# Decoder layer on Trainium2: sample activations of the down stage loaded in three pieces and kept, a fourth sum of w_down made one stage earlier, w_out in another order

## The chip, the cores and the metric

The kernel runs on one core of a Trainium2 chip. TensorE (PE) multiplies matrices, VectorE (DVE), ScalarE (ACT) and GpSimd (POOL) do elementwise work, and SyncE (SP) issues the DMA transfers. Each engine works through its own queue in order, and an instruction starts when those of other engines or DMAs that it needs have signalled. The metric is the device time of one launch in microseconds; lower is better.

## The reference

One layer of a decoder for 1024 prompt tokens and 64 sample tokens, D_MODEL 1024, D_FF 2816. Only the end of the layer matters here:

```
mix = (g_conv * u_out + g_nsa * nsa) @ w_out           # 1024 x 1024
x   = x + g1 * mix
h   = rms_norm(x, ffn_norm_g) * (1 + sc2) + sh2
ffn = (silu(h @ w_gate) * (h @ w_up)) @ w_down         # 1024 x 2816, twice, and 2816 x 1024
y   = x + g2 * ffn
```

All data are fp32.

## The kernel before

Each fp32 operand of a matrix product is split in two parts: `hi`, a rounded copy made by ACT (L152), and `lo = src - hi`, made by DVE or POOL. A product `mm3` is three matmuls (L338, L339, L340: hi·hi, lo·hi, hi·lo). For the 64 sample tokens `mm2` (L343, L344) packs hi and lo of the activations side by side in one left operand of 128 columns.

The three stages at the end:

- **w_out.** `out_half(i, j)` makes 128 tokens (i = 0 to 7; i = 8 is the samples) of one half of 512 columns: 24 matmuls into a `pf` bank, DVE's L1599 (times g1) and L1600 (plus x), a store (L1606), ACT's square with a row sum. When j is 1 the row's norm follows (L1610, L252, POOL's L253) and x is scaled, half by ACT (L152) and half by DVE (L1616). `norm2(sg)` transposes 256 tokens on PE (L1644), applies scale and shift (ACT L1647, DVE L1649) and splits the result (DVE or POOL L158). `norm2s` does the samples.
- **Gate and up.** 22 blocks `t` of 128 columns; blocks kk and kk + 11 form a pair. The product of a 2 by 2 block matrix is made with 7 products instead of 8, so sums of operands are needed on both sides. `build(u)` makes those of the activations, u = 0 for the tokens of groups 0 and 1, u = 1 for groups 2 and 3: 8 subtractions in place (L1675 to L1678) and 4 splits in two views (L1681), for u = 1 a third view for the samples. The splits go to `tq` tiles that take the place of the weights of w_out: `quarter(u)` hands out those of column half u. `load_up(t)` loads four tiles of weights and makes their sums and splits (L1715 on DVE or POOL, L1722, L1723, L1725, L1733). Raw tiles go round a ring `w` of six buffers. Each pair also runs two generators in spare places between the products: `second(kk)` loads three tiles of w_down, makes their sum `t2` (two L1792) and stores it, and `sums(kk)` makes the sums of the activations for the down stage (L1779).
- **Down.** The same scheme with phases p = 1, 2, 6, 7, 5, 4, 3 of 11 steps kk, 12 matmuls each into four banks `p`. `raw_` loads one operand of 256 KB; `parts` splits it, hi on ACT (L152), lo on DVE or POOL (L1891). p = 7 and p = 5 load two tiles of w_down and subtract them (L1958, L1961); p = 4 loads one and `t2` and subtracts (L1964). In p = 1, 2, 7, 3 each kk has two more matmuls (L343, L344) for the samples, whose activations `sample(t)` loads (L1896), copies (ACT L152, `sa`) and splits (L1899): 44 times, each t twice. At the end of a phase its four banks are added to accumulators (ACT's copy after p = 1; DVE's L1998 after p = 6, L2000 after p = 7) and come free for the phase after next but one.

The order of the instructions on each engine is fixed when the program is built: a scheduler simulates the program as written and lists it by its own clock. Tiles with a tag share a ring of `bufs` buffers, and a tile's first write waits for the last use of the tile before it in that buffer.

The lines of the order of w_out, of `place` and of the phases stand below.

Of the kernel before, what the change touches and what calls it, by code (L numbers as in the profile page):

```python
# [123 lines left out]
def emit(tc, I, O):  # L124
    nc = tc.nc
# [1417 lines left out]

    NH = FF // 256
    act_d = {p: T(dp, [NH, 128, 512], f"act_d{p}") for p in range(1, 8)}
    acts_d = T(dp, [2 * NH, 128, 2, 32], "acts_d")
    t2_d = T(dp, [NH, 128, 512], "t2_d")

    def gate_rows(i, pool, tag, bufs):
        out = []  # L1550
# [74 lines left out]
    def place(sg):  # L1625

        u, r = sg // 2, sg % 2
        if r == 0:
            tb[u] = [[quarter(u) for _ in range(2)] for _ in range(4)]
        for a in range(2):  # L1630
            if sg == 0:
                full[u][a] = [T(ap_[0], [128, 2, 256], "aw", bufs=6) for _ in range(2)]
            else:
                x = T(mp, [128, 4, SEG[1 + r * u * 2]], ("qh0", "ql0")[a] + str(1 + r * u * 2))
                full[u][2 * r + a] = [x[:, 2 * b:2 * b + 2, :256] for b in range(2)]
# [30 lines left out]

    def build(u):

        views = [([t[a] for t in full[u]],
                  [[t[:, 2 * a:2 * a + 2, :256] for t in x] for x in tb[u]]) for a in range(2)]  # L1670
        if u:
            views.append(([xs[:, 4 * a:4 * a + 4, 32 * b:32 * b + 32] for a, b in ((0, 0), (1, 0), (0, 1), (1, 1))],
                          [[t[:, :, 256:] for t in x] for x in tb[u]]))
        for (b11, b21, b12, b22), dst in views:
            V.tensor_tensor(b11, b12, b11, op=ALU.subtract)  # L1675
            V.tensor_tensor(b12, b22, b12, op=ALU.subtract)
            V.tensor_tensor(b22, b22, b11, op=ALU.subtract)
            V.tensor_tensor(b21, b21, b22, op=ALU.subtract)  # L1678
            for src, j in ((b22, 1), (b12, 2), (b11, 0), (b21, 3)):
                acopy(dst[j][0], src)  # L1680
                V.tensor_tensor(dst[j][1], src, f(dst[j][0]), op=ALU.subtract)  # L1681

    for i in range(9):
        out_half(i, 0)
    for sg in (0, 1):
        for i in (2 * sg, 2 * sg + 1):
            out_half(i, 1)
        norm2(sg)
    build(0)
    out_half(8, 1)  # L1690

# [95 lines left out]
    def second(kk):  # L1787

        t2 = wd(kk + NH, 1, T(stg[0], [128, 512], "t2", bufs=2))
        for j, op_ in ((1, ALU.subtract), (0, ALU.add)):  # L1790
            b = wd(kk, j, T(fr, [128, 512], "w", bufs=6))
            V.tensor_tensor(t2, t2, b, op=op_)  # L1792
            yield
        nc.sync.dma_start(t2_d[kk], t2)

    todo = []

# [7 lines left out]
    for n_, t in enumerate([a + b for a in range(NH) for b in (0, NH)]):  # L1805
# [8 lines left out]
        for u in range(2):  # L1814
# [32 lines left out]
            if (u, t // NH) != (1, 0):  # L1847
                store({(0, 0): 1, (0, 1): 2, (1, 1): 4}[u, t // NH], kk, h)
            if u:
                nc.sync.dma_start(acts_d[t], h[:, :, 256:])  # L1850
        if t >= NH:
            todo.append(sums(kk))
    while todo:
# [18 lines left out]
    with ExitStack() as es:  # L1872
# [14 lines left out]
        def parts(src, e):  # L1887
# [3 lines left out]
            e.tensor_tensor(lo, src, f(hi), op=ALU.subtract)  # L1891
            return hi, lo

        def sample(t):
            sr = T(dn, [128, 64], "sr", bufs=8)
            nc.sync.dma_start(sr.rearrange("p (a c) -> p a c", a=2), acts_d[t])  # L1896
            sa_ = T(dn, [128, 128], "sa", F32R, bufs=8)
            acopy(sa_[:, :64], sr)
            V.tensor_tensor(sa_[:, 64:], sr, f(sa_[:, :64]), op=ALU.subtract)  # L1899
            return sa_  # L1900

        def load_x2(i, j):
            n = 128 if i < 8 else 64
# [29 lines left out]
        for p in (1, 2, 6, 7, 5, 4, 3):  # L1933
            pd_ = [T(psd, [128, 512], "p", bufs=7) for _ in range(4)]
            if p in (1, 7):
                ps_ = T(psd, [128, 512], "s", bufs=1)
            j, e = (0 if p < 3 else 1), (G if p in (4, 5, 7) else V)

            def step(n, kk, a, b, c):
                if n == 4:  # L1940
                    mm2(ps_, c[0], *c[1], p in (1, 7) and kk == 0, p in (2, 3) and kk == NH - 1)
                else:
                    mm3(pd_[n], a[0][:, n * 128:n * 128 + 128], a[1][:, n * 128:n * 128 + 128], *b,
                        kk == 0, kk == NH - 1)

            late = []
            order = ([4] if p in (1, 2, 7, 3) else []) + list(range(4))
            for kk in range(NH):
                l = raw_(act_d[p][kk])
                c = None  # L1950
                if p in (1, 2, 3):
# [8 lines left out]
                    o_, r = wraw_(kk, 1), wraw_(kk, 0)  # L1960
                    V.tensor_tensor(r, o_, r, op=ALU.subtract)  # L1961
                else:
                    o_, r = wraw_(kk + NH, 0), raw_(t2_d[kk])
                    V.tensor_tensor(r, o_, r, op=ALU.subtract)  # L1964
                a, b = parts(l, e), parts(r, V)
                if p in (1, 2, 3):
                    c = sample(kk + (NH if p > 1 else 0)), b
# [93 lines left out]
```

## Time and profile before

| | us |
|---|---|
| three runs | 1936.15, 1926.62, 1930.79 |
| median | 1930.79 |
| profiled execution | 1924.53 |
| its span | 1922.7 |

| engine | busy us | share |
|---|---|---|
| PE (matmul) | 1822.3 | 95% |
| PEld (weight load) | 1633.5 | 85% |
| DVE | 1479.6 | 77% |
| ACT | 858.5 | 45% |
| POOL | 713.4 | 37% |

The page divides the span into 40 slices. w_out ends and gate/up begins near 1177 us, the down stage runs from about 1645 us to the end. In the rows below a time is in microseconds from the start of the span, and L numbers are lines of the kernel before. `A<-B` is out<-in; a wait in brackets is the engine's idle time just before the row and what ended it.

### The profile page before, as it was taken

How to read it: one execution, taken by the hardware profiler on the slowest of the kernel's cores; microseconds unless marked ns; L12 is line 12 of the kernel's file. 1: busy time of each engine (PE TensorE's matmuls, PEld its weight loads, DVE VectorE, ACT ScalarE, POOL GpSimd, SP SyncE). 2: the span in 40 equal slices, each digit the busy share in tenths (PEclk: the TensorE clock that was granted, in tenths of full speed). 3: DMA queues.
4: the chain of work that ended last, by engine and by line, in shares of the span. 5: the costliest groups of instructions: out<-in, count | busy, mean ns of one | idle time of the engine just before them, and what ended most of it. 6: DMA issues, size and time to landing. Idle time of an engine off the chain costs nothing.

```text
span 1922.7 us, 32565 instructions
## 1 busy us (share of the span) xinstructions
PE 1822.3 (95%) x11432; PEld 1633.5 (85%) x11432; DVE 1479.6 (77%) x2698; ACT 858.5 (45%) x2086; POOL 713.4 (37%) x689
## 2 busy tenths in 40 slices
PE   8999899999999789999998997999999999999899
PEld 3889888888898589788888886999999999877687
DVE  4877799987958875898886538988777888767873
ACT  5434642344444342777784325433323323464440
POOL 3789421144544666555555403211111111002420
PEclk9989999999999889999999998999999999999999
DMA  9576534443454425110006712344433344596862
GB/s 314 181 228 214 164 113 144 140 149 115 150 171 138 155 85 176 55 47 6 1 7 196 225 47 71 106 140 122 123 113 112 111 130 129 181 303 217 277 225 77
DMA packets 228050, 271.86 MB, mean 141 GB/s; under 512 B 32297, under 2 KB 151609, under 8 KB 227814
## 3 DMA queue, kind: packets, MB, share of 16 engines
q1 hardware_dynamic: 218670, 236.22, 38.9%
q0 software_dynamic: 9216, 33.56, 5.2%
q8 instruction: 90, 1.47, 0.3%
q14 instruction: 74, 0.61, 0.1%
HBM read 215.68 MB, written 58.52 MB: 143 GB/s over the span
## 4 chain that ended last, share of the span: by engine, by line
PE 47%; DMA 4%; DVE 4%; issue 1%; POOL 1%; ACT 1%; SPq 0%; DVEq 0%; ACTq 0%; POOLq 0%
PE pf L338 6%; PE pf L340 6%; PE pf L339 6%; PE pt L340 3%; PE pt L339 3%; PE pt L338 3%; PE pT L1400 3%; PE p L338 3%; PE p L340 3%; PE p L339 3%; PE po L1407 2%; PE po L1408 2%; DMA raw<-in_w_down 2%; PE pS L1359 1%; PE pS L1361 1%
## 5 line engine op out<-in xcount | busy, mean ns | idle before, releaser
L338 PE MATMUL pd<-hh,whi 128*128 128x384 f32 (+1 forms) x576 | 192.4, 334 | 1.0 <-ACT stg L152 0.9
L340 PE MATMUL pd<-hh,wlo 128*128 128x384 f32 (+1 forms) x576 | 190.7, 332 | 0.8 <-DVE wlo L270 0.8
L339 PE MATMUL pd<-hl,whi 128*128 128x384 f32 (+1 forms) x576 | 190.5, 331 | 0.0
L1096 DVE SCALAR_TENSOR_TENSOR y<-U,wdT,y 128x1024 f32<-128x1024 f32 x120 | 163.2, 1360 | 0.6
L1715 POOL TENSOR_TENSOR aw<-s,aw 128x512 fp32r<-128x512 f32 x21 | 28.9, 1376 | 305.7 <-ACT aw L152 291.4
L152 ACT ACTIVATE whi<-wraw 128x512 fp32r<-128x512 f32 (+1 forms) x133 | 81.7, 626 | 92.5 <-PE pd L339 40.9
L152 ACT ACTIVATE aw<-w 128x512 fp32r<-128x512 f32 x133 | 83.0, 628 | 88.4 <-PE pf L339 55.5
L958 POOL TENSOR_TENSOR vv<-kraw,vv 128x256 fp32r<-128x256 f32 x80 | 92.3, 1178 | 67.7 <-ACT vv L152 67.6
L338 PEld LDWEIGHTS pd<-hh,whi 128*128 128x128 f32 x576 | 108.7, 189 | 7.6 <-ACT stg L152 1.2
L1388 POOL TENSOR_SCALAR P<-P,ast 128x640 f32<-128x640 f32 (+7 forms) x128 | 88.9, 715 | 70.5 <-DVE ast L1384 66.6
L1404 DVE TENSOR_TENSOR pl<-pT,ph 128x512 fp32r<-128x512 f32 (+1 forms) x148 | 99.2, 681 | 18.0 <-ACT ph L152 16.7
L340 PEld LDWEIGHTS pd<-hh,wlo 128*128 128x128 f32 x576 | 108.5, 188 | 3.9 <-DVE wlo L270 2.2
L339 PEld LDWEIGHTS pd<-hl,whi 128*128 128x128 f32 x576 | 108.6, 189 | 3.0 <-issue 0.5
L338 PE MATMUL pz<-whi,hh 128*128 128x256 f32 (+1 forms) x320 | 96.0, 301 | 14.9 <-ACT zt L152 13.2
L338 PE MATMUL pf<-tq,aw 128*128 128x256 f32 (+1 forms) x352 | 101.8, 289 | 3.5 <-ACT s L152 1.8
L338 PE MATMUL pt<-tq,aw 128*128 128x256 f32 (+1 forms) x352 | 101.9, 290 | 2.1 <-ACT aw L152 2.1
L340 PE MATMUL pt<-tq,aw 128*128 128x256 f32 (+1 forms) x352 | 101.7, 289 | 1.0 <-POOL aw L1715 1.0
L339 PE MATMUL pt<-tq,aw 128*128 128x256 f32 (+1 forms) x352 | 101.9, 290 | 0.0
L340 PE MATMUL pf<-tq,aw 128*128 128x256 f32 (+1 forms) x352 | 101.8, 289 | 0.0
L339 PE MATMUL pf<-tq,aw 128*128 128x256 f32 (+1 forms) x352 | 101.7, 289 | 0.0
L340 PE MATMUL pf<-qh,aw 128*128 128x256 f32 (+1 forms) x352 | 101.5, 288 | 0.0
L339 PE MATMUL pf<-ql,aw 128*128 128x256 f32 (+1 forms) x352 | 101.4, 288 | 0.0
(653 smaller groups left out, 6368.7 us busy)
## 6 DMA issues: line engine op xcount, KB each, us to landing
wraw<-in_w_in SPq DMA_DIRECT2D x68, 256.0 KB
wraw<-in_w_ada SPq DMA_DIRECT2D x64, 256.0 KB
w<-in_w_down SPq DMA_DIRECT2D x62, 256.0 KB
raw<-in_w_down SPq DMA_DIRECT2D x48, 256.0 KB
w<-in_w_gate SPq DMA_DIRECT2D x44, 256.0 KB
w<-in_w_up SPq DMA_DIRECT2D x44, 256.0 KB
raw<-act_d SPq DMA_DIRECT2D x42, 256.0 KB
w<-act_d SPq DMA_DIRECT2D x35, 256.0 KB
```

Of the source, the lines that this page charges most:

```text
L152: S.activation(out, in_, AF.Copy, scale=scale)
L338: PE.matmul(out, ah, bh, start=first, stop=False)
L339: PE.matmul(out, ah, bl, start=False, stop=False)
L340: PE.matmul(out, al, bh, start=False, stop=last)
L958: G.tensor_tensor(vv[:, :, 1], r, f(vv[:, :, 0]), op=ALU.subtract)
L1096: V.scalar_tensor_tensor(op, U[:, k:k + TP], wk, op, op0=ALU.mult, op1=ALU.add)
L1388: G.tensor_scalar(P_[br][g][:, :w], P_[br][g][:, :w], st[:, 2, br, g:g + 1], 1.0, op0=ALU.mult, op1=ALU.mult)
L1400: PE.transpose(pT[:nk, g * 128:(g + 1) * 128], a, ident)
L1404: V.tensor_tensor(pl_[:nk], pT[:nk], f(ph[:nk]), op=ALU.subtract)
L1407: PE.matmul(po, va, ph[:nk], start=(bi == 0), stop=False)
L1408: PE.matmul(po, va, pl_[:nk], start=False, stop=(bi == len(blocks) - 1))
L1715: e.tensor_tensor(lo, src, f(hi), op=ALU.subtract)
```

## The change

1. `acts_d`, the samples' activations in HBM, are laid out as [22, 128, 64]. `load_sample(t, n)` loads n blocks with one DMA, copies them with one ACT instruction and subtracts with one of DVE, into `sal`, which is kept for the whole stage. Three calls in p = 1, before kk = 0, 4 and 7, load 8, 8 and 6 blocks, and `sample(t)` is a view of `sal`.
2. `second(kk)` loads one more tile of w_down into the ring `w`, subtracts `t2` (new line L1800) and stores the result in `t4_d` (L1801). p = 4 loads it from there: its load of w_down and its L1964 are gone. The lo parts of its activations go from POOL to DVE (`e` is POOL for p = 5 and 7 alone).
3. w_out: the halves (0,1), (1,1), norm2(0), (2,1), (3,1), norm2(1) stand between the halves j = 0, and (7,0) and (8,0) stand just ahead of build(0). `tb[u]` is taken in `build` instead of `place`.

Instructions: DVE 2580 rows to 2549, ACT 1715 to 1673, POOL 666 to 656, SP 1089 to 1059, PE 10863 in both. Lines after 1546 move by one to 16: L1599, L1600, L1616, L1649 are L1600, L1601, L1617, L1648; L1681 stays; L1715, L1722, L1733, L1792, L1825 are L1719, L1726, L1737, L1796, L1832; L1891, L1961, L2000 are L1898, L1976, L2014.

```diff
@@ -1543,8 +1543,9 @@
 
     NH = FF // 256
     act_d = {p: T(dp, [NH, 128, 512], f"act_d{p}") for p in range(1, 8)}
-    acts_d = T(dp, [2 * NH, 128, 2, 32], "acts_d")
+    acts_d = T(dp, [2 * NH, 128, 64], "acts_d")
     t2_d = T(dp, [NH, 128, 512], "t2_d")
+    t4_d = T(dp, [NH, 128, 512], "t4_d")
 
     def gate_rows(i, pool, tag, bufs):
         out = []
@@ -1625,8 +1626,6 @@
     def place(sg):
 
         u, r = sg // 2, sg % 2
-        if r == 0:
-            tb[u] = [[quarter(u) for _ in range(2)] for _ in range(4)]
         for a in range(2):
             if sg == 0:
                 full[u][a] = [T(ap_[0], [128, 2, 256], "aw", bufs=6) for _ in range(2)]
@@ -1666,6 +1665,7 @@
 
     def build(u):
 
+        tb[u] = [[quarter(u) for _ in range(2)] for _ in range(4)]
         views = [([t[a] for t in full[u]],
                   [[t[:, 2 * a:2 * a + 2, :256] for t in x] for x in tb[u]]) for a in range(2)]
         if u:
@@ -1680,12 +1680,16 @@
                 acopy(dst[j][0], src)
                 V.tensor_tensor(dst[j][1], src, f(dst[j][0]), op=ALU.subtract)
 
-    for i in range(9):
+    for i in range(4):
         out_half(i, 0)
-    for sg in (0, 1):
-        for i in (2 * sg, 2 * sg + 1):
-            out_half(i, 1)
-        norm2(sg)
+    for i, j in ((0, 1), (1, 1), (4, 0)):
+        out_half(i, j)
+    norm2(0)
+    for i, j in ((2, 1), (3, 1), (5, 0), (6, 0)):
+        out_half(i, j)
+    norm2(1)
+    out_half(7, 0)
+    out_half(8, 0)
     build(0)
     out_half(8, 1)
 
@@ -1792,6 +1796,9 @@
             V.tensor_tensor(t2, t2, b, op=op_)
             yield
         nc.sync.dma_start(t2_d[kk], t2)
+        b = wd(kk + NH, 0, T(fr, [128, 512], "w", bufs=6))
+        V.tensor_tensor(b, b, t2, op=ALU.subtract)
+        nc.sync.dma_start(t4_d[kk], b)
 
     todo = []
 
@@ -1847,7 +1854,7 @@
             if (u, t // NH) != (1, 0):
                 store({(0, 0): 1, (0, 1): 2, (1, 1): 4}[u, t // NH], kk, h)
             if u:
-                nc.sync.dma_start(acts_d[t], h[:, :, 256:])
+                nc.sync.dma_start(acts_d[t].rearrange("p (a c) -> p a c", a=2), h[:, :, 256:])
         if t >= NH:
             todo.append(sums(kk))
     while todo:
@@ -1891,13 +1898,17 @@
             e.tensor_tensor(lo, src, f(hi), op=ALU.subtract)
             return hi, lo
 
+
+        sal = T(dn, [128, 2 * NH, 2, 64], "sal", F32R)
+
+        def load_sample(t, n):
+            r = T(fr, [128, 512], "w", bufs=6)[:, :64 * n].rearrange("p (t c) -> p t c", t=n)
+            nc.sync.dma_start(r, acts_d[t:t + n].rearrange("t p c -> p t c"))
+            acopy(sal[:, t:t + n, 0], r)
+            V.tensor_tensor(sal[:, t:t + n, 1], r, f(sal[:, t:t + n, 0]), op=ALU.subtract)
+
         def sample(t):
-            sr = T(dn, [128, 64], "sr", bufs=8)
-            nc.sync.dma_start(sr.rearrange("p (a c) -> p a c", a=2), acts_d[t])
-            sa_ = T(dn, [128, 128], "sa", F32R, bufs=8)
-            acopy(sa_[:, :64], sr)
-            V.tensor_tensor(sa_[:, 64:], sr, f(sa_[:, :64]), op=ALU.subtract)
-            return sa_
+            return sal[:, t].rearrange("p e c -> p (e c)")
 
         def load_x2(i, j):
             n = 128 if i < 8 else 64
@@ -1934,7 +1945,7 @@
             pd_ = [T(psd, [128, 512], "p", bufs=7) for _ in range(4)]
             if p in (1, 7):
                 ps_ = T(psd, [128, 512], "s", bufs=1)
-            j, e = (0 if p < 3 else 1), (G if p in (4, 5, 7) else V)
+            j, e = (0 if p < 3 else 1), (G if p in (5, 7) else V)
 
             def step(n, kk, a, b, c):
                 if n == 4:
@@ -1943,9 +1954,13 @@
                     mm3(pd_[n], a[0][:, n * 128:n * 128 + 128], a[1][:, n * 128:n * 128 + 128], *b,
                         kk == 0, kk == NH - 1)
 
+            if p == 1:
+                load_sample(0, 8)
             late = []
             order = ([4] if p in (1, 2, 7, 3) else []) + list(range(4))
             for kk in range(NH):
+                if p == 1 and kk in (4, 7):
+                    load_sample(*((8, 8), (16, 6))[kk == 7])
                 l = raw_(act_d[p][kk])
                 c = None
                 if p in (1, 2, 3):
@@ -1960,8 +1975,7 @@
                     o_, r = wraw_(kk, 1), wraw_(kk, 0)
                     V.tensor_tensor(r, o_, r, op=ALU.subtract)
                 else:
-                    o_, r = wraw_(kk + NH, 0), raw_(t2_d[kk])
-                    V.tensor_tensor(r, o_, r, op=ALU.subtract)
+                    r = raw_(t4_d[kk])
                 a, b = parts(l, e), parts(r, V)
                 if p in (1, 2, 3):
                     c = sample(kk + (NH if p > 1 else 0)), b
```

DVE at the end of w_out, before: `tq` are the splits of build(0) (L1681), `xt<-pf` is the eviction of an out_half (the first below that of (6,1)).

```order
L1599 TENSOR_TENSOR xt_13764<-pf_13739,indgp_12909 128x512
L1681 TENSOR_TENSOR tq_2877_13324<-aw_13331,tq_2876_13323 128x512
L1681 TENSOR_TENSOR tq_2877_13324<-aw_13332,tq_2876_13323 128x512
L1610 TENSOR_TENSOR rs_2814_12904<-ssq_2813_12903 128x1
L1616 TENSOR_SCALAR x_2924_13596<-x_2919_13558,rs_2814_12904 128x512
L1681 TENSOR_TENSOR tq_2883_13330<-aw_13333,tq_2882_13329 128x512
L1681 TENSOR_TENSOR tq_2883_13330<-aw_13334,tq_2882_13329 128x512
L252 SCALAR_TENSOR_TENSOR rs_2814_12904<-rs_2814_12904,ck_61 128x1
L1715 TENSOR_TENSOR aw_13726<-w_13715,aw_13725 128x512
L1715 TENSOR_TENSOR aw_13733<-w_13717,aw_13732 128x512
L1616 TENSOR_SCALAR x_2930_13636<-x_2925_13598,rs_2814_12904 128x512
L1600 TENSOR_TENSOR x_2961_13737<-x_2961_13737,xt_13764 128x512
```

The same place after, from the scaling of (5,1) to the eviction of (7,1); `xt<-pf` of L1600 is first that of (6,1), then that of (7,1):

```order
L1617 TENSOR_SCALAR x_2931_13637<-x_2926_13599,rs_2815_12905 128x512
L1600 TENSOR_TENSOR xt_13757<-pf_13732,indgp_12910 128x512
L1601 TENSOR_TENSOR x_2954_13730<-x_2954_13730,xt_13757 128x512
L1611 TENSOR_TENSOR rs_2815_12905<-ssq_2814_12904 128x1
L252 SCALAR_TENSOR_TENSOR rs_2815_12905<-rs_2815_12905,ck_61 128x1
L1617 TENSOR_SCALAR x_2959_13768<-x_2954_13730,rs_2815_12905 128x512
L1648 TENSOR_SCALAR qh_2932_13639<-pt_13641,A_23_88,B_24_89 128x256
L1648 TENSOR_SCALAR qh_2932_13639<-pt_13653,A_23_88,B_24_89 128x256
L158 TENSOR_TENSOR ql_2691_12311<-qh_2932_13639,qh_2683_12303 128x256
L1600 TENSOR_TENSOR xt_13797<-pf_13772,indgp_12910 128x512
```

The splits of build(0) (eight in all, the last four here), two splits of weights (L1715) and a sum (L1733, the row behind the ones shown) stood in DVE's queue between the evictions of (6,1) and (7,1). The splits now end 28 rows ahead of the eviction of (7,1), before that of (8,1); the two splits of weights and the sum stand beside that of (8,1).

DVE at the end of p = 7 before: the last subtraction of p = 5 (L1961) and one split stand just ahead of these rows, and the first eviction of p = 7 (L2000) ends them; L1964 is the subtraction of p = 4, L1899 the split of a sample block:

```order
L1899 TENSOR_TENSOR sa_21846<-sr_21844,sa_21846 128x64
L1964 TENSOR_TENSOR raw_21431<-raw_21429,raw_21431 128x512
L1891 TENSOR_TENSOR tq_2878_13325<-w_21349,tq_2878_13325 128x512
L1899 TENSOR_TENSOR sa_21873<-sr_21871,sa_21873 128x64
L1964 TENSOR_TENSOR raw_21454<-raw_21452,raw_21454 128x512
L1964 TENSOR_TENSOR w_21477<-w_21475,w_21477 128x512
L1891 TENSOR_TENSOR tq_2880_13327<-raw_21372,tq_2880_13327 128x512
L1891 TENSOR_TENSOR tq_2876_13323<-raw_21431,tq_2876_13323 128x512
L1899 TENSOR_TENSOR sa_21900<-sr_21898,sa_21900 128x64
L1964 TENSOR_TENSOR w_21500<-w_21498,w_21500 128x512
L1891 TENSOR_TENSOR qh_2685_12305<-raw_21454,qh_2685_12305 128x512
L2000 TENSOR_TENSOR qh_3963_19879<-p_20773,qh_3961_19877 128x512
```

The same place after (L1976, L1898, L2014):

```order
L1976 TENSOR_TENSOR raw_21265<-w_21263,raw_21265 128x512
L1898 TENSOR_TENSOR qh_2681_12301<-w_21219,qh_2681_12301 128x512
L1898 TENSOR_TENSOR tq_2909_13496<-w_21242,tq_2909_13496 128x512
L1898 TENSOR_TENSOR tq_2911_13498<-raw_21265,tq_2911_13498 128x512
L1898 TENSOR_TENSOR tq_2912_13499<-raw_21320,tq_2912_13499 128x512
L1898 TENSOR_TENSOR tq_2907_13494<-raw_21322,tq_2907_13494 128x512
L1898 TENSOR_TENSOR tq_2908_13495<-raw_21340,tq_2908_13495 128x512
L1898 TENSOR_TENSOR qh_2685_12305<-raw_21342,qh_2685_12305 128x512
L2014 TENSOR_TENSOR qh_3975_19924<-p_20721,qh_3973_19922 128x512
```

Between the last subtraction of p = 5 and the eviction stood 12 instructions before, four of them subtractions of p = 4 on two loads each and three splits of samples; after, 7 splits.

## Rows read from the trace of the kernel before

**Rows 1.** The page's engines: busy us, share, instructions.

```profile
PE 1822.3 (95%) x11432; PEld 1633.5 (85%) x11432; DVE 1479.6 (77%) x2698; ACT 858.5 (45%) x2086; POOL 713.4 (37%) x689
```

**Rows 2.** Stretches: busy PE, PEld, DVE, ACT, POOL; granted clock; DMA.

```profile
1100.00:1140.00 40.00, 40.00 (x176) 32.69 (x175) 13.62 (x24) 7.87 (x20) 0.98 (x2) 1.00 0.16 57
1170.00:1230.00 60.00, 47.40 (x301) 42.73 (x300) 58.08 (x115) 35.45 (x79) 22.11 (x16) 0.86 0.33 104
1190.00:1200.00 10.00, 5.10 (x23) 3.55 (x22) 10.00 (x25) 8.30 (x22) 3.90 (x5) 0.55 0.22 78
1300.00:1600.00 300.00, 300.00 (x2399) 300.00 (x2398) 239.38 (x485) 96.07 (x188) 42.01 (x29) 1.00 0.39 119
1818.00:1829.00 11.00, 4.99 (x13) 3.61 (x12) 10.80 (x15) 4.65 (x9) 4.86 (x4) 0.70 0.96 335
```

**Rows 3.** What PE waited for, 1176 to 1226: us in total, times, longest.

```profile
PE pt L1644 <- ACT x L152: 5.0, 3, 2.3
PE pt L338 <- ACT aw L152: 2.1, 2, 1.2
PE pf L338 <- ACT s L152: 1.8, 1, 1.8
PE pf L338 <- ACT aw L152: 1.7, 1, 1.7
PE pt L340 <- POOL aw L1715: 1.0, 1, 1.0
```

**Rows 4.** Timeline of PE there: start, us, instruction, idle before.

```profile
1177.17 0.28 PE L338 MATMUL pf<-qh,aw 128*128 128x256 f32 x1
...
1199.64 0.58 PE L338 MATMUL pt<-tq,aw 128*128 128x256 f32 x1 [1.22 <-ACT aw L152]
...
1221.43 0.30 PE L340 MATMUL pt<-qh,aw 128*128 128x288 f32 x1
```

**Rows 5.** Timeline of DVE there.

```profile
1179.61 1.28 DVE L1681 TENSOR_TENSOR tq<-aw,tq 128x512 fp32r<-128x512 f32 x2
...
1185.88 0.68 DVE L1599 TENSOR_TENSOR xt<-pf,indgp 128x512 f32<-128x512 f32 x1
...
1192.19 0.14 DVE L1610 TENSOR_TENSOR rs<-ssq 128x1 f32<-128x1 f32 x1
...
1206.08 1.78 DVE L1792 TENSOR_TENSOR t<-t,w 128x512 f32<-128x512 f32 x1
...
1216.20 0.68 DVE L1681 TENSOR_TENSOR tq<-ql,tq 128x512 fp32r<-128x512 f32 x1
```

**Rows 6.** What PE waited for, 1660 to 1920.

```profile
PE p L338 <- DVE qh L2000: 6.0, 1, 6.0
PE p L338 <- DVE qh L1998: 3.1, 1, 3.1
PE p L338 <- ACT qh L152: 1.5, 1, 1.5
```

**Rows 7.** Timeline of DVE at the end of p = 7.

```profile
1811.88 1.02 DVE L1961 TENSOR_TENSOR raw<-w,raw 128x512 f32<-128x512 f32 x1 [1.93 <-POOL ql L1891]
...
1817.79 0.69 DVE L1964 TENSOR_TENSOR raw<-raw,raw 128x512 f32<-128x512 f32 x1 [1.34 <-DMA raw<-t_d]
...
1821.79 1.53 DVE L1964 TENSOR_TENSOR w<-w,w 128x512 f32<-128x512 f32 x1 [0.15 <-DMA w<-t_d]
...
1823.84 0.68 DVE L2000 TENSOR_TENSOR qh<-p,qh 128x512 f32<-128x512 f32 x1
```

**Rows 8.** Timeline of ACT at the end of p = 1.

```profile
1707.25 0.63 ACT L152 ACTIVATE ql<-w 128x512 fp32r<-128x512 f32 x1 [2.87 <-DMA w<-act_d]
...
1710.70 1.06 ACT L152 ACTIVATE qh<-p 128x512 f32<-128x512 f32 x2
```

**Rows 9.** Gate/up: line L1792, count, shortest, median and longest ns.

```profile
L1792 DVE TENSOR_TENSOR t<-t,w x22: 675/686/1778, 1201.6 to 1628.0; 128x512 f32<-128x512 f32 x22
```

**Rows 10.** What DVE waited for most, 1300 to 1600.

```profile
DVE s L1722 <- DMA w<-in_w_up: 18.8, 13, 2.9
```

## The prediction

> **What bounds the kernel now.** I read the page's engines first: PE is busy 95% of the span, the next engine 77% [rows 1]. So time is won only where PE stands still or works at a lowered clock, and the second step is to ask for the stretches of those stages that the diff touches. Gate/up from 1300 to 1600 leaves nothing: PE is busy 300.00 of 300 us at clock 1.00, beside a DVE of 239.38 [rows 2]. Most of w_out is the same, 176 matmuls in 40 us, 0.227 us each, with DVE at a third [rows 2]. Two places differ.
>
> The first is the passage from w_out to gate/up. From 1170 to 1230 PE is busy 47.40 us at a mean clock of 0.86 [rows 2]: 47.40 x 0.86 = 40.8 us of work at full clock in 60, a loss of 19.2 us. DVE is busy 58.08 us of the same 60. The list of PE's waits there sums to 11.6 us, mostly for ACT's `x` and `aw` [rows 3]; the rest of the loss is the clock, 0.55 in the worst stretch [rows 2]. ACT has 35 us of work in 60 [rows 2], so it is not the one that is late; it waits for what DVE gives it.
>
> The second is the down stage. Three waits carry its loss: 6.0 us for DVE's L2000 (from p = 7 to p = 5), 3.1 for DVE's L1998 (p = 6 to p = 7), 1.5 for ACT (p = 1 to p = 2) [rows 6]. In the 11 us around the first of them PE runs 13 matmuls [rows 2]; at 0.227 us these are 2.95 us of work, so that place loses 8.0 us: its wait, and 2 us at the clock that follows it (0.70 over the stretch).
>
> **The change part by part.**
>
> *Order of w_out.* Let T be 1177.17, where the first gate/up matmul follows the last of w_out [rows 4]. The eviction of the last half (7,1), L1599, starts at 1185.88 [rows 5], 8.7 us behind T: DVE still has the splits of build(0) to do (the two at 1179.61 among them) and three operations on weights. From that eviction hangs a chain: x, its norm, the transposes of norm2(3), the memory for the second pool of weight tiles (PE's 1.22 at 1199.64 [rows 4]), build(1). The last split of build(1) ends at 1216.20 + 0.68 = 1216.88, T + 39.7, and the last product that needs it at 1221.43 + 0.30 [rows 4, 5]. From the eviction to that split are 31.0 us, with 59 instructions of DVE. In the new order all of build(0) stands ahead of the eviction of (8,1), where in the order before DVE was two thirds idle (13.62 us of 40) [rows 2], so that it costs nothing there; the loads of x, the splits of w_out's second half and the weights' buffers are all ready by then, as the halves of j = 0 that are moved behind keep PE as full as before. The eviction of (7,1) then follows its last matmul at about T + 0.4. Behind it, to the last split of build(1), 57 instructions stand, of nearly the same forms: two evictions of transposes (L1649) and one scaling fewer, two L1825, one L1723 and the new subtraction L1800 more. I take the 31.0 us again: T + 31.4, 8.3 sooner. I take 8. The lower end is 4: what stood in DVE's queue also covered the wait for the norm (L1610 came 3 us behind the half's last elementwise step, at 1192.19 [rows 5]); with the cover gone DVE idles there, and L1800 waits for a load that itself waits for a buffer `w`. The upper end is 12, if PE, waiting less, also keeps its clock.
>
> A rule of the Trainium skill, page "SBUF — State Buffer", section "Who interferes with whom", bears on this place: VectorE and GpSimd share a pair of ports to SBUF under an exclusive lock, and the one that has it stops the other. The trace agrees: L1792 takes 0.686 us in the median and 1.778 at most [rows 9], the latter at 1206.08 [rows 5]. L1800 is such an instruction with two inputs in SBUF; by the rule it would cost 1.8 instead of 0.7 us in front of the last splits, and the sum would be 7 instead of 8.
>
> *Fourth sum.* Per pair one 256 KB load, one DVE subtraction and one 256 KB store more in gate/up: 11 x 0.69 = 7.5 us of DVE, 11 x 1.78 = 20 at most [rows 9]. A pair lasts some 42 us, and DVE's share of idle time, 20% [rows 2], is 8 us of it, so 0.7 to 1.8 us are covered, as long as L1800 doesn't wait long for its load: it stands in DVE's queue ahead of sums that PE's banks wait for. The nearest row for such a wait is L1722's for w_up, 18.8 us over 13 times, 2.9 at most [rows 10], with no wait of PE in that stretch [rows 2]. DMA moves 119 GB/s there, a third of the 335 that it reaches elsewhere [rows 2]. I take +0.5 for this and for the start of p = 1, where `sal` and its first copy stand ahead of other work on ACT; bounds -0.5 and +3.
>
> *p = 7 to p = 5.* PE's last matmul of p = 7 ends near 1818.6; the eviction L2000 that frees p = 5's last bank starts at 1823.84. DVE is what is late: between the last subtraction of p = 5 at 1811.88 and the eviction stand 12 instructions, four of them L1964 that wait for DMA (1.34 at 1817.79) or run slowly (1.53 at 1821.79) [rows 7]. In the new order 7 splits stand there. They take 7 x 0.6 to 7 x 0.7 us, 4.9 at most where none runs beside POOL; from 1812.9 that gives 1817.8, before the last matmul. What is late next is the eviction itself: PE waits some 0.7 us for it, and may lose a little clock. So 7 of the 8.0 us go. Those splits need four loads of p = 4 where there were twelve. DMA moves 335 GB/s here [rows 2], 0.78 us for 256 KB: the four land in 3 us, inside the same time. Lower end 3: the 1.93 us wait for POOL's `ql` at 1811.88 [rows 7] stays, p = 5 has three loads per kk as before and takes all that DMA gives. The 11 lo parts that go from POOL to DVE cost 11 x 0.7 on DVE in a phase whose L1964, 11 x 0.7, go.
>
> *p = 1 to p = 2.* ACT's copy of the banks, at 1710.70, stands behind splits of p = 2, one of which waited 2.87 us for its load [rows 8]. By the new order six splits fewer stand ahead of it, so six loads fewer have to land: 6 x 0.78 us. That is more than the 1.5 of the wait. I take 1.5; lower end 0, as the three merged loads bring all 22 blocks in p = 1 instead of 11 and a few.
>
> *p = 6 to p = 7.* The order there stays; DVE waits for the loads of p = 7. I take 0 of its 3.1.
>
> Sum: -8 - 7 - 1.5 + 0.5 = -16. The profiled execution took 1924.53, so 1908.5. It is 6.3 below the median of the runs, 1930.79; against that the same sum gives 1914.8. **I predict 1915.** All the lower ends together give -4 - 3 + 0 + 3 = -4, 1927; all the upper ends -12 - 8 - 1.5 - 0.5 = -22, 1909.
>
> **The rivals.** A measurement of this kernel can tell from no change about 0.5%, 9.7 us: faster means below 1921.1.
>
> *The stall of p = 7 stays.* DMA, not the queue of DVE, sets the end of p = 7: p = 5's loads land no sooner, and its last subtraction still comes near 1812 or later. For it: the DMA share of 0.96 over the 11 us [rows 2] and the wait for DMA at 1817.79 [rows 7]. Against: the last subtraction of p = 5 came 11 us ahead of the eviction. Then -8 - 1.5 + 0.5 = -9, 1922.
>
> *The passage gives nothing.* DVE is full from 1170 to 1230, and the chain from the last half to build(1) keeps its length by itself (transposes at the lowered clock, ACT's splits, the memory of the second weight pool), or the moved halves starve PE earlier, as w_out's j = 1 weights are wanted sooner. For it: PE's largest wait, 5.0 us, is for the scaled x [rows 3], which needs the norm whatever the order. Against: the eviction ran 8.7 us late, which no latency explains. Then -7 - 1.5 + 0.5 = -8, 1923.
>
> *Slower.* The third load of w_down takes its place in the ring of six buffers, where a pair now takes eleven buffers instead of ten; its buffer comes free late, L1800 holds DVE's queue, and the next weights wait for the store of `t4`. PE then stops once a pair for lack of splits or banks. It decides from the point at which DVE's delay exceeds the 8 us that a pair leaves it. At a wait of PE of 2.2 us per pair the 11 pairs cost 24, and 24 - 16 = +8: 1939. At 1.5 us per pair the gains are just eaten. For it: DVE's waits for w_up [rows 10] show that loads through this ring are late already. Against: they never reached PE in 300 us [rows 2].
>
> **How the numbers follow.** My forecast, 1909 to 1921, has 0.50; a larger gain, the clock kept through the passage and the stall before p = 7 shortened too, 0.08; the stall of p = 7 stays 0.15; the passage gives nothing 0.17; slower 0.10. Faster by over 0.5%: 0.48 + 0.08 + 0.06 + 0.06 = 0.68, since the two middle rivals lie just outside the bound and each falls inside it in four cases of ten; within 0.5%: 0.24; slower: 0.08. The range 1905 to 1928 takes in both middle rivals and leaves out the slow one and a gain beyond 26 us; the forecast's own range is 1909 to 1921.
>
> **What would show it.** Right: the eviction of (7,1) within 1 us of its last matmul, the last L1681 near T + 31, PE's sum of waits in the passage down from 11.6 to about 6; no wait over 2 us for L2014 and none for ACT after p = 1; 3 us before p = 7 as now; no wait of PE between 1300 and 1600. Wrong: a wait at L2014 above 4 us (DMA), a last L1681 beyond T + 37 (the chain), or PE waits that return once a pair in gate/up.

## The result and the profile after

| | before | after |
|---|---|---|
| median of three runs, us | 1930.79 | 1910.56 |
| lowest to highest | 1926.62 to 1936.15 | 1904.04 to 1911.73 |
| profiled execution, its span | 1924.53, 1922.7 | 1911.73, 1910.0 |

The ratio is 0.9893, with a 95% interval of 0.9858 to 0.9929: 20 us less, where 16 were forecast, 1910.6 against 1915.

The time is best followed on PE, which does the same work in both. The starts of its first and last matmul of each stage, read from the timelines, give these lengths (us). "Passage" is from the first gate/up matmul, T, to the 504th, the end of the third block of weights in the order of work; from there to the last, 3192 matmuls later, is gate/up. A phase of the down stage, with the step into it, is counted from the last matmul into a `p` bank of the phase before to its own last.

| stage | before | after | difference |
|---|---|---|---|
| up to the first w_out matmul | 1074.17 | 1075.80 | +1.6 |
| w_out, first to last matmul | 102.76 | 108.45 | +5.7 |
| passage | 87.65 | 76.85 | -10.8 |
| gate/up, the rest | 399.00 | 399.00 | 0.0 |
| down: p = 1 | 38.11 | 37.83 | -0.3 |
| p = 2, with the step into it | 37.29 | 35.49 | -1.8 |
| p = 6, with the step into it | 30.16 | 29.92 | -0.2 |
| p = 7, with the step into it | 40.47 | 40.97 | +0.5 |
| p = 5, with the step into it | 38.39 | 30.01 | -8.4 |
| p = 4 and p = 3 | 65.25 | 65.25 | 0.0 |

The stages that the forecast had named give -10.8 - 8.4 - 1.8 + 0.5 - 0.3 = -20.8, about what the medians show. The profiled execution shows 12.7 less in its span, mostly because its w_out took 5.7 us longer. Held against the kernel before matmul by matmul, 4.8 of the 5.7 us arise near the start of w_out, where PE worked at half clock in two places. The other 0.9 us are work that changed sides: in the new order eight of the 16 transposes of norm2(2) stand ahead of the last w_out matmul (40 transposes in w_out instead of 32, 24 instead of 32 in the passage). So 0.9 of the passage's 10.8 us are moved, not won.

**The passage.** Stretches of the kernel after (busy PE, PEld, DVE, ACT, POOL; granted clock; DMA):

```profile
1170.00:1230.00 60.00, 54.67 (x359) 49.32 (x358) 52.47 (x110) 30.62 (x70) 15.30 (x15) 0.94 0.34 105
1300.00:1600.00 300.00, 300.00 (x2402) 300.00 (x2401) 244.76 (x493) 94.86 (x188) 42.94 (x30) 1.00 0.44 133
```

Of the same 60 us PE now uses 54.67 at a clock of 0.94, against 47.40 at 0.86 [rows 2]. T lies 7.3 us later in this execution; 60 us cut at the same distance from T as before (1177.3 to 1237.3) give the same 54.67 and 0.94. The second row, 1300 to 1600, shows what the fourth sum costs: DVE 5.4 us busier in 300, DMA at 133 instead of 119 GB/s, PE still without a gap.

The passage itself, first of the kernel before, then after:

```profile
1177.17:1264.82 87.65, 75.05 (x545) 71.74 (x543) 82.02 (x168) 42.38 (x92) 24.62 (x17) 0.90 0.36 110
```

```profile
1184.48:1261.33 76.85, 71.52 (x537) 68.86 (x536) 72.22 (x147) 34.21 (x75) 16.34 (x13) 0.96 0.39 123
```

PE stands idle 5.3 us of it instead of 12.6, and is busy 3.5 us less: 0.9 for the eight transposes, the rest mostly because the transposes that stay ran 0.11 us apart at full clock, where many before ran 0.21 apart at half clock.

PE's largest waits in the passage of the kernel after (1140 to 1240; us in total, times, longest):

```profile
PE pt L338 <- ACT aw L152: 2.4, 2, 1.5
PE pf L338 <- ACT s L152: 0.9, 1, 0.9
```

The wait for the scaled x, 5.0 us and the largest before [rows 3], is gone. The timelines say why. Below are the first gate/up matmul, the eviction of (7,1) and the last splits of build(1), PE first, then DVE:

```profile
1184.48 0.28 PE L338 MATMUL pf<-qh,aw 128*128 128x256 f32 x1
```

```profile
1184.68 0.69 DVE L1600 TENSOR_TENSOR xt<-pf,indgp 128x512 f32<-128x512 f32 x1
...
1214.24 0.68 DVE L1681 TENSOR_TENSOR tq<-ql,tq 128x512 fp32r<-128x512 f32 x1
1214.84 0.28 DVE L1681 TENSOR_TENSOR tq<-xs,tq 128x128 fp32r<-128x128 f32 x1
```

The eviction starts 0.2 us behind T instead of 8.7, and the last split ends at T + 30.6 instead of T + 39.7 [rows 4, 5].

**The down stage.** Of the three waits [rows 6] one is left (1660 to 1920):

```profile
PE p L338 <- DVE qh L2012: 3.6, 1, 3.6
```

It is the one from p = 6 to p = 7. Just ahead of that eviction DVE waits for a load of w_down:

```profile
1774.03 0.69 DVE L1976 TENSOR_TENSOR w<-w,w 128x512 f32<-128x512 f32 x1 [0.91 <-DMA w<-in_w_down]
1774.64 0.68 DVE L2012 TENSOR_TENSOR qh<-p,qh 128x512 f32<-128x512 f32 x1
```

DVE at the end of p = 7 after, to be held against [rows 7]:

```profile
1806.49 0.69 DVE L1976 TENSOR_TENSOR raw<-w,raw 128x512 f32<-128x512 f32 x1 [0.99 <-issue]
1807.10 1.79 DVE L1898 TENSOR_TENSOR qh<-w,qh 128x512 fp32r<-128x512 f32 x1
1808.81 0.68 DVE L1898 TENSOR_TENSOR tq<-w,tq 128x512 fp32r<-128x512 f32 x1
1809.42 2.49 DVE L1898 TENSOR_TENSOR tq<-raw,tq 128x512 fp32r<-128x512 f32 x4
1811.82 0.68 DVE L1898 TENSOR_TENSOR qh<-raw,qh 128x512 fp32r<-128x512 f32 x1
1812.43 0.68 DVE L2014 TENSOR_TENSOR qh<-p,qh 128x512 f32<-128x512 f32 x1
```

From the last subtraction of p = 5 to the eviction are 5.9 us instead of 12, without a wait between, and PE has no wait there. The one split that takes 1.79 us lies beside the one instruction that POOL has there:

```profile
1806.54 1.81 POOL L1898 TENSOR_TENSOR tq<-w,tq 128x512 fp32r<-128x512 f32 x1 [2.79 <-PE s L343]
```

ACT at the end of p = 1 after: its copies of the banks (`qh<-p`) now stand among splits whose loads have landed, against [rows 8].

```profile
1701.09 0.60 ACT L152 ACTIVATE qh<-p 128x512 f32<-128x512 f32 x1 [1.17 <-PE p L340]
1701.58 0.63 ACT L152 ACTIVATE qh<-w 128x512 fp32r<-128x512 f32 x1
1702.10 0.59 ACT L152 ACTIVATE qh<-p 128x512 f32<-128x512 f32 x1
```

**The cost in gate/up.** The two waits of DVE that answer to [rows 10]:

```profile
DVE s L1726 <- DMA w<-in_w_up: 11.4, 10, 2.2
...
DVE w L1800 <- DMA w<-in_w_down: 5.6, 7, 1.9
```

L1800 does wait for its load, up to 1.9 us, but the two together are no more than w_up's alone before (17.0 against 18.8), and none of it reaches PE, which has no wait from 1300 to 1600.

### The profile page after: what moved, and what is told of

The parts are those of the page before. It is cut to its first block, busy times and chain, and to the rows that moved or that the text cites. A ratio compares the mean times of both kernels' runs of the same rounds, so it can differ in the third digit from the quotient of the medians.

```text
span 1910.0 us, 32401 instructions
## 1 busy us (share of the span) xinstructions
PE 1822.7 (95%) x11432; PEld 1633.7 (86%) x11432; DVE 1472.3 (77%) x2668; ACT 852.4 (45%) x2045; POOL 693.6 (36%) x678
## 5 line engine op out<-in xcount | busy, mean ns | idle before, releaser
L1719 POOL TENSOR_TENSOR aw<-s,aw 128x512 fp32r<-128x512 f32 x21 | 29.4, 1400 | 309.9 <-ACT aw L152 236.3
L152 ACT ACTIVATE aw<-w 128x512 fp32r<-128x512 f32 x133 | 82.3, 627 | 76.7 <-PE pf L339 44.4
L958 POOL TENSOR_TENSOR vv<-kraw,vv 128x256 fp32r<-128x256 f32 x80 | 85.8, 1097 | 69.4 <-ACT vv L152 69.3
L338 PE MATMUL pz<-whi,hh 128*128 128x256 f32 (+1 forms) x320 | 95.0, 299 | 15.5 <-ACT zt L152 13.9
L338 PE MATMUL pf<-tq,aw 128*128 128x256 f32 (+1 forms) x352 | 101.3, 288 | 1.2 <-ACT s L152 0.9
L340 PE MATMUL pf<-qh,aw 128*128 128x256 f32 (+1 forms) x352 | 101.3, 288 | 0.0
L339 PE MATMUL pf<-tq,aw 128*128 128x256 f32 (+1 forms) x352 | 101.2, 288 | 0.0
L338 PE MATMUL pf<-qh,aw 128*128 128x256 f32 (+1 forms) x352 | 101.2, 287 | 0.0
```

Source lines behind the costliest of these rows:

```text
L152: S.activation(out, in_, AF.Copy, scale=scale)
L338: PE.matmul(out, ah, bh, start=first, stop=False)
L339: PE.matmul(out, ah, bl, start=False, stop=False)
L340: PE.matmul(out, al, bh, start=False, stop=last)
L958: G.tensor_tensor(vv[:, :, 1], r, f(vv[:, :, 0]), op=ALU.subtract)
```

## Experiments

Each edit is to the kernel before or to the changed one, as said. Ratios are to the kernel before, with 95% intervals. All stage times are from the profiles.

**The parts one at a time.** To the kernel before, the order of w_out alone (with `tb[u]` taken in `build`), the fourth sum alone (with `e` for p = 4), the sample pieces alone.

> Only the new order of w_out with build taking its tiles itself; sample loads and w_down sums as before. Theory (each part has its own place): the passage from w_out to gate/up wins 9 to 11 us, counted from the first gate/up matmul to the start of block t = 2; the three waits of the down stage stay as before (6.0, 3.1 and 1.5 us, within 1 us each). Total about -9 against before, or -4 if the lowered clock behind the gate matmuls at the start of w_out, 5.7 us, shows again. Rival (the DVE time won by the other two parts makes the passage): the passage wins under 5 us.

> Only the fourth sum of w_down in gate/up, with the lo parts of p = 4 on DVE; order of w_out and sample loads as before. Theory: the wait from p = 7 to p = 5 falls from 6.0 to under 1.5 us and the low clock behind it goes, -7 us; nothing at the other places, passage within 2 us of before; total -7. Rival (the sample blocks are half of it: their 44 small loads and three of the 12 instructions): the wait stays above 3 us, total -3 or less.

> Only the samples' activations in three pieces, kept. Theory: the wait from p = 1 to p = 2 (1.5 us) goes, the one from p = 7 to p = 5 falls by 1 to 2 us (three instructions fewer of 0.2 to 1.3 us), total -1.5 to -4. Rival: it carries the gain of the down stage, wait from p = 7 to p = 5 under 2 us, total -8.

| | before | order | sum | samples | all (two profiles) |
|---|---|---|---|---|---|
| ratio | | 0.9935 (0.9909 to 0.9961) | 0.9975 (0.9957 to 0.9992) | 0.9955 (0.9938 to 0.9971) | 0.9893, 0.9868 |
| passage | 87.65 | 76.69 | 89.28 | 88.67 | 76.85, 76.79 |
| p = 1 | 38.11 | 41.13 | 37.82 | 36.94 | 37.83, 35.36 |
| p = 2 and step | 37.29 | 35.49 | 35.49 | 35.49 | 35.49, 35.49 |
| p = 6 and step | 30.16 | 30.45 | 34.33 | 29.92 | 29.92, 29.92 |
| p = 7 and step | 40.47 | 39.85 | 39.66 | 36.21 | 40.97, 42.79 |
| p = 5 and step | 38.39 | 38.44 | 30.45 | 39.57 | 30.01, 29.92 |
| down in all | 249.67 | 250.62 | 243.00 | 243.38 | 239.47, 238.74 |

PE's largest waits in the down stage, first the order alone, then the sum, then the samples:

```profile
PE p L338 <- DVE qh L2003: 5.6, 1, 5.6
PE p L338 <- DVE qh L2001: 2.5, 1, 2.5
PE p L338 <- ACT tq L152: 1.7, 1, 1.7
```

```profile
PE p L338 <- DVE xt L1930: 2.5, 1, 2.5
PE p L338 <- DVE qh L2001: 2.3, 1, 2.3
```

```profile
PE p L338 <- DVE qh L2008: 7.2, 1, 7.2
PE p L338 <- DVE qh L2006: 0.5, 1, 0.5
```

The passage belongs to the order of w_out and the step into p = 5 to the fourth sum, each whole. The order alone won 12.5 us by its ratio, more than the 9 expected, but 9 lies inside its interval.

The sum alone won 4.8 us by its ratio, where 7 were expected. Its profile has the 7.9 us at the step into p = 5, but also 4.2 us lost in p = 6, by a wait behind p = 2 (2.5) that came in; the down stage as a whole won 6.7.

The sample pieces alone won 8.7 us by their ratio, more than the 1.5 to 4 expected; their profile has 6.3 us in the down stage. Nothing of it comes from the wait out of p = 7, where 1 to 2 us were expected: it grew to 7.2. The largest piece is 4.3 us in p = 7, and that is not there when all three parts are together (40.97, 42.79).

The wait of ACT before p = 2 is gone with the samples alone, but it is gone with the order alone and with the sum alone as well, and p = 2 takes 35.49 us in all three. The 1.7 us for ACT in the first list above lie elsewhere, at 1670.8 in the first steps of p = 1. So this experiment does not show which part takes that wait away.

**Is it build(0)?** The changed kernel, build(0) written later.

```diff
-    build(0)
     out_half(8, 1)
 ...
         if sg == 3:
+            build(0)
             next(up0)
```

> The changed kernel with build(0) written behind norm2(2) and the samples' norm instead of ahead of the half (8,1); all else as changed. Theory (the splits of build(0) in DVE's queue behind the last w_out matmul are what the passage lost): the eviction of (7,1) starts 4 us or more behind its last matmul and the passage loses 5 to 10 us against the changed kernel. Rival (the order of the halves and the early norm2(1) do it, build(0) is hidden anyway): within 2 us of the changed kernel, the eviction within 1 us of its matmul.

Passage 76.81 us, ratio 0.9888 (0.9864 to 0.9911): the rival's numbers. But the scheduler had put the splits at the same place of DVE's queue as in the changed kernel, ahead of the eviction of (8,1). The text was moved and the work was not, so this tells nothing of either. To move the work, its input has to come later:

```diff
-    norm2(1)
     out_half(7, 0)
     out_half(8, 0)
-    build(0)
     out_half(8, 1)
+    out_half(4, 1)
+    norm2(1)
+    build(0)
 ...
-            out_half(i, 1)
+            if i > 4:
+                out_half(i, 1)
```

> The changed kernel with norm2(1) and build(0) put behind the half (4,1), so that, as before the change, the splits of build(0) stand in DVE's queue between the evictions of (5,1), (6,1) and (7,1); norm2(0) and the halves keep the new places. Theory (these splits behind the last w_out matmul are what the passage lost): from the first gate/up matmul to block t = 2, 76.8 us in the changed kernel and 87.7 before, 84 us or more; the eviction of (7,1) 4 us or more late. Rival (the earlier norm2(0) or other order does it): under 79.

DVE of that kernel, whose last w_out matmul starts at 1176.04:

```profile
1174.57 0.68 DVE L1600 TENSOR_TENSOR xt<-pf,indgp 128x512 f32<-128x512 f32 x1
1175.17 1.28 DVE L1681 TENSOR_TENSOR tq<-aw,tq 128x512 fp32r<-128x512 f32 x2
1176.83 1.28 DVE L1681 TENSOR_TENSOR tq<-aw,tq 128x512 fp32r<-128x512 f32 x2
...
1181.44 0.68 DVE L1600 TENSOR_TENSOR xt<-pf,indgp 128x512 f32<-128x512 f32 x1
...
1212.24 0.68 DVE L1681 TENSOR_TENSOR tq<-ql,tq 128x512 fp32r<-128x512 f32 x1
```

The splits of build(0) stand between the last evictions again, that of (7,1) is 5.4 us late, the last split ends 36.9 us behind the last w_out matmul, and the passage takes 84.57 us. Of the 10.8 us won, 7.8 are lost again by this one step; ratio 0.9917 (0.9880 to 0.9953). Here too 0.9 us are only moved, as the eight transposes stand behind T again (32 in w_out, which took 102.75 us), so 6.9 of 9.9 us are really lost. So it is DVE's backlog of norm2(1) and build(0) that the passage had lost most of its time to.

**DVE's queue loaded and relieved.** In the changed kernel eight maxima of the samples' normed activations `xs` with themselves, which leave the values as they are:

```diff
             norm2s()
+            for _ in range(8):
+                V.tensor_tensor(xs, xs, xs, op=ALU.max)
```

> The changed kernel with eight elementwise maxima of the samples' sums with themselves (128x512 each, value unchanged) added on DVE behind the samples' norm, some 0.6 us each, 4.8 in all, in the stretch behind the last w_out matmul. Theory (DVE's queue is what sets the passage): the time from the first gate/up matmul to block t = 2 grows by 4 to 6 us. Rival (latency of the chain through ACT, PE and the weights' memory sets it, DVE only looks full): it grows by under 2 us.

```profile
1216.93 0.61 PE L338 MATMUL pf<-tq,aw 128*128 128x288 f32 x1 [16.54 <-ACT tq L152]
```

```profile
1215.20 0.68 DVE L1753 TENSOR_TENSOR xs<-xs 128x512 f32<-128x512 f32 x1
...
1217.18 0.75 DVE L1681 TENSOR_TENSOR tq<-xs,tq 128x128 fp32r<-128x128 f32 x3
```

The first row is PE's, the next two are DVE's. Passage 92.32 us, 15.5 more; both forecasts were too low. The ratio is 0.9955 (0.9933 to 0.9977), with a median of 1918.54 us against 1904.20 for the changed kernel in the same series. The eight were not laid down together: work of the next blocks stands between them in DVE's queue, and the samples' share of build(1), which the first products of u = 1 need, comes at 1215.9 behind the last. The direction is the theory's; the size is that of the order in the queue, not of the added work.

The relief, on top of a further kernel (below): the samples' norm written right behind (8,1), which the scheduler did follow, so that its operations come ahead of the eviction of (7,1).

> The kernel with the differences for p = 5 and p = 7 kept, and besides the samples' norm written right behind the half (8,1) instead of behind norm2(2), so that its five DVE operations come before the last w_out matmul. Theory (DVE sets the passage): passage 77.7 us there, 74 to 76 here, total -2 to -3. Rival (chain latency): within 1 us.

Passage 75.39 against 77.67, as the theory had it, but 0.8 of these 2.3 us are again only moved: the samples' eight transposes now stand in w_out, which grows by that much. And 77.67 is the longest passage of the new order without added work; the seven others take 76.7 to 76.9, against which only 0.5 to 0.7 us are left. So this step does not decide between the theory and its rival. Ratio 0.9848 (0.9817 to 0.9879); a gain of this size can't be told in the time.

**The 11 lo parts of p = 4.** In the changed kernel `e` is POOL for p = 4, 5 and 7, as before the change.

> The changed kernel with the lo parts of p = 4's activations on POOL again. Theory (off the path): the step from p = 7 to p = 5 stays without a wait over 1 us, total within 1.5 us of the changed kernel. Rival (the DVE that POOL slows was a part of the stall): the wait for the eviction of p = 7 comes back with 2 us or more.

DVE, POOL and PE of that kernel at the end of p = 7, one fence each:

```profile
1800.25 1.78 DVE L1898 TENSOR_TENSOR qh<-w,qh 128x512 fp32r<-128x512 f32 x1
1801.96 1.78 DVE L1898 TENSOR_TENSOR tq<-w,tq 128x512 fp32r<-128x512 f32 x1
1803.67 3.49 DVE L1898 TENSOR_TENSOR tq<-raw,tq 128x512 fp32r<-128x512 f32 x2
1807.08 1.74 DVE L1898 TENSOR_TENSOR qh<-raw,qh 128x512 fp32r<-128x512 f32 x1
1808.75 1.28 DVE L2014 TENSOR_TENSOR qh<-p,qh 128x512 f32<-128x512 f32 x2
```

```profile
1799.70 1.79 POOL L1898 TENSOR_TENSOR tq<-w,tq 128x512 fp32r<-128x512 f32 x1 [2.70 <-PE p L339]
1801.66 3.25 POOL L1898 TENSOR_TENSOR tq<-raw,tq 128x512 fp32r<-128x512 f32 x2 [0.17 <-ACT tq L152]
1804.86 3.42 POOL L1898 TENSOR_TENSOR ql<-raw,ql 128x512 fp32r<-128x512 f32 x2
```

```profile
1809.48 0.50 PE L338 MATMUL p<-tq,tq 128*128 128x512 f32 x1 [2.70 <-DVE qh L2014]
```

The rival held. Beside POOL's splits all five of DVE's take 1.7 to 1.8 us, where six of seven took 0.6 to 0.7 in the changed kernel; five splits take 8.5 us. The wait is back with 2.7 us and p = 5 with its step takes 34.55 us instead of 29.92. So of the 8.4 us, 4.6 come from taking POOL away from DVE's side and 3.8 from the subtractions and loads that are gone. Ratio 0.9908 (0.9880 to 0.9936).

**What the samples' part is worth.** The changed kernel without it.

> The changed kernel with the samples' loads as before the change (44 loads, copies and splits). Theory by the runs so far (the step out of p = 7 belongs to the fourth sum alone, and the samples' part only moves the waits before p = 2 and p = 7): wait out of p = 7 under 1 us; down stage 1 to 4 us longer than the 238.7 to 241.3 of the changed kernel. Rival: the samples' part is worth nothing with the others there, down stage within 1 us.

```profile
PE p L338 <- DVE qh L2004: 2.6, 1, 2.6
PE p L338 <- ACT qh L152: 2.4, 1, 2.4
```

Down stage 242.69, 1.4 to 6.2 us longer than with it (236.5 to 241.3 in five profiles whose down stage is that of the changed kernel); none of the waits is at the end of p = 7. The wait of ACT before p = 2 is back with 2.4 us, and p = 2 with its step takes 39.76 us instead of 35.49. As the wait was also absent with the old loads in two experiments above, p = 1 and p = 2 are better taken together: 73.3 to 77.9 us in the four kernels with the old loads, 70.9 to 73.4 in the ten with the new. Ratio 0.9891 (0.9855 to 0.9927), too wide to tell 3 us.

**A version that goes on.** The difference for p = 5 alone, or those for p = 5 and p = 7, made in gate/up too and loaded. For p = 5:

```diff
 ...
+        V.tensor_tensor(b1, b1, b0, op=ALU.subtract)
+        nc.sync.dma_start(t5_d[kk], b1)
+        yield
+        V.tensor_tensor(t2, t2, b1, op=ALU.subtract)
 ...
-                    o_, r = wraw_(kk, 1), wraw_(kk, 0)
-                    V.tensor_tensor(r, o_, r, op=ALU.subtract)
+                    r = raw_(t5_d[kk])
```

> The changed kernel with the difference of w_down for p = 5 alone kept from gate/up; p = 7 loads two tiles and subtracts as before. It tells which subtraction held the eviction of p = 6. If it was p = 5's, which stands right ahead of it in DVE's queue, the wait before p = 7 falls under 1 us, as when both are kept (0). If it was p = 7's own, with loads that came 1.7 to 2.0 us late, 2 us or more stay.

> Goes on from the changed kernel: gate/up also stores the differences of w_down that p = 7 and p = 5 need, so that p = 5 has two loads per step and no subtraction and p = 7 no subtraction; 11 subtractions and 22 stores more in gate/up. Theory (what is left before p = 7, a wait of 3.6 us and 1.7 us at half clock, is the eviction of p = 6 held in DVE's queue behind subtractions that wait for loads): the wait falls under 1 us, total -4 to -5 against the changed kernel. Rival 1 (the loads of p = 7, still three per step, set it): wait stays at 3 us or more, total -1 to 0. Rival 2 (the ring of six buffers holds weights back in gate/up): PE waits appear between the products, total +3 or more.

With both, PE has no wait in the down stage at all, which takes 233.04 us instead of 236.5 to 241.3, and gate/up still 399.00. With p = 5's alone a wait of 1.8 is left:

```profile
PE p L338 <- DVE qh L2015: 1.8, 1, 1.8
```

It lies between the two forecasts: neither subtraction alone held the eviction. The ratios are 0.9835 (0.9800 to 0.9869) for p = 5 alone and 0.9852 (0.9829 to 0.9875) for both, 1899.73 and 1901.10 us, against 0.9868 (0.9842 to 0.9894) and 1904.20 for the changed kernel in the same series as the latter. The profiles show the gain; the times don't separate the three.

**The changed kernel again.**

> The changed kernel again, unaltered, for a second profile and a closer ratio. Theory (the 5.7 us that its first profile loses at the start of w_out, at half clock behind the gate matmuls, come and go with the execution): the time from the first to the last w_out matmul, 102.8 us before and 108.5 in the first profile, comes out elsewhere between 102.5 and 108.5. Rival (the new order costs them): 108 again. All other stretches within 1 us of the first profile; ratio 0.985 to 0.993.

w_out took 105.23 us, as the theory had it. Two other stretches differ from the first profile by more than the 1 us expected: p = 1 took 2.5 us less and p = 7 1.8 us more. The first row below is of the kernel before, then after, then after again, 1074 to 1110:

```profile
1074.00:1110.00 36.00, 35.83 (x148) 27.59 (x149) 14.58 (x20) 11.44 (x26) 7.54 (x9) 1.00 0.64 204
```

```profile
1074.00:1110.00 36.00, 34.20 (x120) 25.50 (x121) 14.86 (x20) 11.26 (x25) 9.10 (x12) 0.86 0.67 205
```

```profile
1074.00:1110.00 36.00, 34.07 (x137) 26.13 (x136) 15.19 (x22) 11.86 (x28) 9.24 (x12) 0.95 0.68 211
```

The granted clock is 1.00, 0.86 and 0.95. (The counts of matmuls also differ because w_out starts 1.6 and 2.9 us later in the second and third row.) The kernels with the old order of w_out took 102.8, 104.3 and 106.0 us, those with the new order of halves 102.8 to 108.5. Matmul by matmul against the kernel before, what is lost near the start of w_out is 0 to 4.8 us and comes with half clock, in kernels of either order. What the new order adds is 0.9 us at the end of w_out, the same in both profiles of the changed kernel and in the order alone, and not there in norm1_3, which has 32 transposes in w_out as before. So the order costs w_out the 0.9 us of transposes that the passage no longer has, and nothing ties the other 4.8 of the 5.7 us to it.

## Why the prediction was right

The likeliest case came in, with the two large steps where they were put, and the time is 4.4 us below the forecast. Part of that was luck: at the step into p = 5 over half of the gain came from a move that the forecast had valued at nothing.

- *Passage, -8: -10.8, of which 0.9 is moved into w_out.* The eviction at T + 0.2 (forecast 0.4), the last split at T + 30.6 (31.4), the waits 5.3 (about 6), where the five largest before were 11.6 and all together 12.4. The 31.0 us from eviction to last split stayed 30.4, as taken over. Of the other 9.9 us, 7.3 are idle time of PE and 2.6 busy time, for which the upper end had named the reason: PE, waiting less, also kept more of its clock (0.96 against 0.90 over the passage). The kernel with norm2(1) and build(0) later gave 6.9 us back, so the mechanism is shown.
- *The price of L1800, 1.8 us instead of 0.7.* All 11 took 0.675 to 0.694 us. POOL had no instruction running beside any of them, so the price was not due, and this place tests nothing. The Trainium skill, "SBUF — State Buffer", section "Who interferes with whom", says that a VectorE instruction with two inputs in SBUF contends with a GpSimd instruction that reads SBUF. The trace of p4_pool agrees, at the end of p = 7, with 1.7 to 1.8 us for each of five splits beside POOL's and 2.7 us of wait for PE.
- *Step from p = 7 to p = 5, -7: -8.4.* 7 splits, then the eviction, and no wait of PE: right. Two readings of that step were wrong. The lo parts moved from POOL to DVE were set against the L1964 that go and valued at nothing; they are over half of the gain (4.6 of 8.4), and the 4.9 us "where none runs beside POOL" came near (5.3) only because of that move. And 1818.6 is not where p = 7's last matmul ends: that one starts at 1814.32, and up to 1818.6 PE does 17 matmuls of p = 5 that don't need the bank. That is why the eviction, 3.3 us behind the start of p = 7's last matmul in the kernel after (1812.43 against 1809.10), costs PE nothing.
- *Step from p = 1 to p = 2, -1.5: -1.8.* The size is right. That the samples' part does it is not shown: the wait returns in the changed kernel without it, but it is also gone with the order alone and with the sum alone.
- *Step into p = 7, 0: +0.5.* Right in this profile; the four others with the same down stage have 1.4, 4.4, 4.5 and 4.7 us of wait, and p = 7 takes 37.2 to 43.2 us over the five. The eviction stands behind subtractions that wait for loads of w_down, and keeping p = 5's and p = 7's differences takes that wait away. Why the loads land so differently from kernel to kernel, and why the samples alone had only 0.5 us of wait there, stays open.
- *Gate/up and the start of p = 1, +0.5: 0.0 and -0.3.* The slower rival's wait is there (L1800, up to 1.9 us), but it stays inside DVE's slack: gate/up took 399.00 us in every kernel, even with two stores and a subtraction more per pair.

## What to carry over

Before valuing a queue's backlog, find the last instruction that the next stage waits for, and count what stands ahead of it on its engine; work with early inputs that stands there is worth moving even at some rearranging of another stage. A scheduler may ignore where work is written: to move it, move what it depends on, and look at the order. An elementwise split on POOL can cost twice, in its own time and in DVE's beside it (1.8 instead of 0.7 us here), so count it where DVE is what is waited for, not by its engine. Where a change moves work across the line between two stages, count that work before calling the shorter stage a gain.

## What was not expected of the hardware

Right behind the small matmuls on 19 partitions in w_out (L1562, L1563; eight in 3.7 us before, 4.2 in the first profile after) PE worked at half clock, 1.2 GHz, in some executions and at full clock, 2.4 GHz, in others. In the first profile after, the matmuls behind them are 0.427 us apart from 1091.7 to 1096.4, and in the second from 1090.8 to 1093.8; before, they are 0.227 apart from about 1087.7 on. The code there is the same. Half clock followed in 11 of the 14 profiles and cost 1.5 to 1.6 us in nine of them and 3.2 in two. In three profiles, the first after among them, half clock came at the very start of w_out as well (1076.4 to 1079.4 there) and cost 1.6 us more; PE had waited 2.3 to 2.5 us just before, and 1.2 to 2.0 us in the other eleven. Together the two make the 4.8 us that the first profile after lost. What decides whether the clock falls behind the small matmuls stays open.
